# Joint projection of V and the global queries in the second layer as a 2x2 scheme of seven products

## The chip, the cores and the metric

The kernel runs on one core of a Trainium2 chip. Time is device time in microseconds, from the first to the last instruction of one execution and what lies around it. The engines are TensorE (PE in the profile: matmuls; PEld its weight loads), VectorE (DVE), ScalarE (ACT), GpSimd (POOL) and SyncE (SP), which here issues nearly all DMA transfers.

## The reference

Two layers of an encoder trunk over 512 tokens of width 1024. Each layer adds three things to x: a mixer, a cross attention over 256 memory tokens, and a gated feed-forward part with a convolution of width 3. Only the mixer's projection is touched by the change:

```python
def hybrid_mixer(h, w_in, rpb, q_norm, k_norm, w_out, rows, cos, sin):
    proj = h @ w_in                       # h = rms_norm(x), (512, 1024) @ (1024, 2304)
    na_q, na_k, na_v, g_q, g_k, g_v = jnp.split(proj, IN_SPLIT_POINTS, axis=-1)
    na_out = neighbourhood_attention(na_q, na_k, na_v, rpb, rows)
    g_q = apply_axial_rope(rms_norm(g_q, q_norm), cos, sin)
    g_k = apply_axial_rope(rms_norm(g_k, k_norm), cos, sin)
    gqa_out = gqa_block_attention(g_q, g_k, g_v)
    return jnp.concatenate([na_out, gqa_out], axis=-1) @ w_out
```

na_q, na_k, na_v and g_q have 512 columns each, g_k and g_v 128 each. All is float32.

## The kernel before, in words

**Precision.** A float32 operand is split in two parts, hi (a rounded copy, made on ACT) and lo (the remainder, a subtraction on DVE or POOL). A product is three matmuls: hi x hi, hi x lo, lo x hi (`mm3`, L650).

**Order of the work.** Each engine operation is first recorded on a tape in program order. A planner (`Tape.run`, L270, `Tape.plan`, L373) then lists the operations anew for each engine by estimated costs and due times; TensorE may run ahead of the recorded order within a reach of 300 of its instructions, tiles of the tags mm, r, t and s may be opened somewhat out of order, and all others (raw, hi, lo, sc, tr) only in order. The planner's model knows that some operations of DVE and POOL hold each other up (`Step.shared`, L337 to L340).

**Weights.** `weights()` (L1835) lists all blocks in the order of use. `get_w` (L616) keeps loads ahead: three buffers for raw blocks (N_RAW), four each for hi and lo (N_W). `emit_split` (L591) turns a raw block into hi and lo; its letter says how: "P" takes the remainder on POOL, "D" on DVE, "A" only keeps the raw block for its successor, "B" forms the combinations of the feed-forward scheme. A block is 512 KB.

**Mixer of the second layer.** The last matmuls of the first layer's feed-forward part write x, and `Norm` (L758) keeps x times the gain as hi and lo in two tiles of the tag xg; the norm's factor itself is applied later. `project_qk` (L948) projects pairs of heads, in the order of `NA_ORDER` (L50): q0, k0, q1, k1, then V, then q2, k2, q3, k3. Between q0 and k0 the statistics of the norm are begun (`mix.stat`, L793), after k0 the factor is spread over all rows (`mix.spread`, L804), and only then the first results leave PSUM. `project_v` (L1006) holds x as the stationary operand and streams the weights, 512 columns at a time: four blocks of 128 tokens, 8 chunks of the input width, three matmuls each. `gqa_project_q` (L1199) does the same for the global queries, later, behind `gqa_project_kv`; each block then goes through `head_norm` (L1147), rotation and a transpose.

All projections are pieces of a filler (`Filler`, L1377). `attn_fill.step(N_FIRST[l])` (L1381) runs the first 22 pieces in the second layer ahead of everything else: q0, k0, q1, k1 and six pieces of V. The rest is woven between the steps of the neighbourhood attention (`weave`, L1395; 2050 ns of TensorE work at each of three places of a step, NA_FILL), and then between those of the global attention (L1402). The output projection of the neighbourhood half opens once the last of its heads is there.

**Buffers.** PSUM has four banks of the tag mm, two of sc, two of tr. SBUF has 23 tiles of the tag r and 14 of the tag t.

**A scheme of the same kind** is there already: the feed-forward part computes gate and value with seven products of half size in place of eight (`operands`, L1557, `up`, L1603), with 128 x 128 weights as the stationary operand.

Of the kernel before, what the change touches and what calls it, by code (L numbers as in the profile page):

```python
# [14 lines left out]
ALU = mybir.AluOpType  # L15
# [4 lines left out]
P = 128  # L20
# [34 lines left out]
NA_FILL = 2050  # L55
# [4 lines left out]
N_RAW, N_W, AHEAD, AHEAD_HELD, N_WARM, N_LATE, N_FIRST = 3, 4, 2, 5, 7, 4, (12, 22)  # L60
# [121 lines left out]
class Tape:  # L182
# [87 lines left out]
    def run(self, due, rank, patience, ahead, margin=0.0, aside={}, order=None, rng=None):  # L270
# [32 lines left out]
        for _ in steps:  # L303
            best = None
            for e in ENGINES:
# [194 lines left out]
def encoder_kernel(ctx: ExitStack, tc: tile.TileContext, t: dict, out: list):  # L500
# [5 lines left out]
    LO_A, SUMS, LO_S = DVE, POOL, DVE  # L506

# [44 lines left out]
    done = [0]  # L552

# [37 lines left out]
    def emit_split(act=ACT, cuts=2):  # L591
# [10 lines left out]
        raws[n] = None  # L602
        if key[0] in ("up", "down", "memq", "memo"):
            cuts = 1
# [85 lines left out]
    def load_parameters():  # L690
        SP.dma_start(par, t["par"])
        taps = par[:, :, CW : CW + 6 * NF].rearrange("p l (i s j) -> p l i s j", i=3, s=2)
        for i in range(DEPTH):
            DVE.tensor_scalar(minus[:, i].rearrange("p (i j) -> p i j", i=3), taps[:, i, :, 1], -1.0, None, op0=ALU.mult)
        SP.dma_start(qkg, t["qkg"])
        SP.dma_start(gcol, t["gcol"])
# [215 lines left out]
    for l in range(DEPTH):  # L912
# [201 lines left out]

        gq, gr, gk, gvt, gtab = [None] * NB, [None] * NB, [], [None] * NB, []
# [31 lines left out]
        def head_norm(x, n, which, b):  # L1147
# [7 lines left out]
            if which:  # L1155
                DVE.scalar_tensor_tensor(view(v), view(v), 1.0 / HD, geps[:, 1, b].unsqueeze(2).to_broadcast([P, 2, 2]),
                                         op0=ALU.mult, op1=ALU.add)
            else:
                DVE.tensor_scalar(v, v, geps[:, 0, b : b + 1], None, op0=ALU.add)
# [217 lines left out]
        attn_fill = Filler(  # L1377
            PE, late, *([project_first(), *units[3:]] if l == 0 else units), gqa_project_kv(), gqa_project_q(),
# [7 lines left out]
        def na_quanta(s):  # L1386
# [4 lines left out]
            if s == 3:  # L1391
                gqa_tables()
            return [NA_FILL] * 3

# [158 lines left out]
        H = S // 2  # L1553
# [281 lines left out]
def weights():  # L1835
# [14 lines left out]

    def pair(j):
# [9 lines left out]
    for l in range(DEPTH):  # L1861
        for n, p in NA_ORDER:
            if n == "v":
# [6 lines left out]
        blocks += wide("gq", "w_in", 1536)  # L1870
# [95 lines left out]
```

## Time and profile before

| | |
|---|---|
| median of 2 runs | 1301.22 us (1300.8 to 1301.65) |
| the profiled execution's own time | 1302.85 us |
| its span in the profile | 1300.8 us |
| mean granted TensorE clock | 0.998 |
| TensorE matmuls | 7557 |
| DMA | 137.48 MB, mean 106 GB/s |
| HBM read and written | 126.18 MB and 2.10 MB |

A line of a timeline has the start in us, the duration, engine, line of the kernel, operation, the tile written and those read, shapes, and the count of merged instructions; in brackets the idle time before it and what ended it. Since the tape plays all operations at one place, every instruction has the line L405; one goes by the names of tiles. In a group of instructions the columns behind the bar are busy time in us and the mean in ns, and behind the second bar idle time before them. In the list of waits stand the engine and tile that waited, what it waited for, and then total us, times, and the longest. Durations of neighbouring instructions on an engine overlap by some tens of ns, so the distance of their starts is what one costs.

### The profile page before, as it was taken

How to read it: one execution, taken by the hardware profiler on the slowest of the kernel's cores; microseconds unless marked ns; L12 is line 12 of the kernel's file. 1: busy time of each engine (PE TensorE's matmuls, PEld its weight loads, DVE VectorE, ACT ScalarE, POOL GpSimd, SP SyncE). 2: the span in 40 equal slices, each digit the busy share in tenths (PEclk: the TensorE clock that was granted, in tenths of full speed). 3: DMA queues.
4: the chain of work that ended last, by engine and by line, in shares of the span. 5: the costliest groups of instructions: out<-in, count | busy, mean ns of one | idle time of the engine just before them, and what ended most of it. 6: DMA issues, size and time to landing. Idle time of an engine off the chain costs nothing.

```text
span 1300.8 us, 20807 instructions
## 1 busy us (share of the span) xinstructions
PE 1290.8 (99%) x7557; PEld 1138.5 (88%) x7557; DVE 1076.1 (83%) x2001; ACT 784.4 (60%) x1526; POOL 659.5 (51%) x527
## 2 busy tenths in 40 slices
PE   9999999999999999999999999999999999999998
PEld 7898888888899999999888988888888999999997
DVE  7689885769999999888555897956799999997884
ACT  7776786555665555554537866865646555554552
POOL 4565857716823534433726566765365333452360
PEclk9999999999999999999999999999999999999999
DMA  8741313313224333223355322232132233323231
GB/s 286 224 141 49 105 56 98 98 35 113 81 82 123 105 113 115 66 98 123 112 162 179 115 80 82 65 99 96 49 98 81 82 115 115 128 99 98 97 99 66
DMA packets 42902, 137.48 MB, mean 106 GB/s; under 512 B 5040, under 2 KB 8496, under 8 KB 42800
## 3 DMA queue, kind: packets, MB, share of 16 engines
q1 hardware_dynamic: 42224, 135.51, 32.9%
q8 instruction: 59, 0.97, 0.3%
q10 hardware_dynamic: 576, 0.66, 0.1%
q14 instruction: 43, 0.35, 0.1%
HBM read 126.18 MB, written 2.10 MB: 99 GB/s over the span
## 4 chain that ended last, share of the span: by engine, by line
PE 91%; DVE 5%; issue 2%; POOL 2%; ACT 1%; DVEq 0%; POOLq 0%; ACTq 0%
PE mm L405 52%; PE tr L405 20%; PE sc L405 19%; DVE t L405 2%; DVE r L405 1%; POOL lo L405 1%; DVE lo L405 0%; DVE s L405 0%; POOL s L405 0%; POOL t L405 0%; ACT r L405 0%; ACT t L405 0%; DVE mm L405 0%; DVE xg L405 0%; DVE hi L405 0%
## 5 line engine op out<-in xcount | busy, mean ns | idle before, releaser
L405 POOL TENSOR_TENSOR lo<-raw,hi 128x512 fp32r<-128x512 f32 (+2 forms) x164 | 255.9, 1579 | 161.6 <-ACT hi L405 153.9
L405 PE MATMUL mm<-xg,hi 128*128 128x512 f32 (+1 forms) x930 | 289.7, 392 | 0.0
L405 POOL TENSOR_TENSOR t<-raw,raw 128x512 f32<-128x512 f32 x64 | 99.1, 1569 | 284.2 <-DMA raw<-in_w 231.1
L405 ACT CAST hi<-raw 128x512 fp32r<-128x512 f32 (+2 forms) x212 | 159.6, 779 | 109.2 <-issue 37.2
L405 PE MATMUL mm<-r,hi 128*128 128x512 f32 (+1 forms) x704 | 222.0, 388 | 0.0
L405 PEld LDWEIGHTS mm<-xg,hi 128*128 128x128 f32 x930 | 170.8, 189 | 31.9
L405 PE MATMUL mm<-xg,lo 128*128 128x512 f32 (+1 forms) x465 | 181.3, 390 | 0.0
L405 PEld LDWEIGHTS mm<-r,hi 128*128 128x128 f32 x704 | 130.2, 188 | 25.9 <-DVE xg L405 0.8
L405 PE MATMUL mm<-r,lo 128*128 128x512 f32 (+1 forms) x384 | 141.5, 369 | 0.0
L405 PE MATMUL sc<-r,r 128*128 128x256 f32 (+1 forms) x760 | 133.9, 309 | 0.0
L405 PE MATMUL sc<-r,hi 128*128 128x256 f32 (+1 forms) x832 | 122.9, 291 | 0.8 <-DVE hi L405 0.8
L405 PEld LDWEIGHTS sc<-r,hi 128*128 128x128 f32 x832 | 109.0, 192 | 3.6 <-DVE hi L405 1.0
L405 PEld LDWEIGHTS sc<-r,r 128*128 128x128 f32 x760 | 106.0, 191 | 6.3 <-ACT t L405 0.6
L405 PE MATMUL tr<-r,lo 128*128 128x256 f32 (+1 forms) x784 | 108.9, 285 | 0.0
L405 PE MATMUL mm<-hi,xg 128*128 128x512 f32 (+1 forms) x384 | 108.1, 357 | 0.0
L405 POOL TENSOR_TENSOR t<-t,raw 128x512 f32<-128x512 f32 x64 | 102.7, 1605 | 5.0
L405 PEld LDWEIGHTS mm<-xg,lo 128*128 128x128 f32 x465 | 87.5, 188 | 18.2
L405 POOL TENSOR_SCALAR t<-t,s 128x512 f32<-128x512 f32 (+1 forms) x112 | 66.9, 611 | 71.7 <-DVE s L405 68.4
L405 PE MATMUL tr<-r,r 128*128 128x256 f32 x768 | 102.7, 283 | 0.0
L405 PEld LDWEIGHTS tr<-r,r 128*128 128x128 f32 x768 | 98.9, 191 | 2.6
L405 PEld LDWEIGHTS tr<-r,lo 128*128 128x128 f32 x784 | 99.7, 192 | 0.8
L405 DVE TENSOR_TENSOR r<-raw,r 128x512 fp32r<-128x512 f32 x96 | 91.3, 956 | 0.2 <-ACT r L405 0.2
(160 smaller groups left out, 2697.3 us busy)
## 6 DMA issues: line engine op xcount, KB each, us to landing
raw<-in_w SPq DMA_DIRECT2D x207, 512.0 KB, 3.5
r<-r SPq DMA_DIRECT2D x30, 256.0 KB, 3.6
r<-in_bias SPq DMA_DIRECT2D x16, 384.0 KB, 4.6
raw<-in_w SPq DMA_DIRECT2D x8, 384.0 KB, 3.1
r<-in_memT SPq DMA_DIRECT2D x4, 512.0 KB, 6.7
xT<-in_w SPq DMA_DIRECT2D x7, 256.5 KB, 4.5
r<-in_w SPq DMA_DIRECT2D x9, 128.0 KB, 4.1
t<-in_memT SPq DMA_DIRECT2D x4, 256.0 KB, 6.1
```

The source lines that it names most:

```text
L405: call(*args, **kwargs)
```

## The change

In the second layer alone, V (512 columns) and the global queries (512 columns) are computed together. The tokens are cut in two halves, the input width in two halves, and the columns in V and queries. Of this 2x2 product of 2x2 blocks, seven products of block size are taken in place of eight. Each has two blocks of 128 tokens by 512 columns, over four chunks of the input width. The left-hand names are combinations of weight blocks, the right-hand ones of blocks of x: 11 x 11, s1 x t1, s2 x t2, 12 x 21, s4 x 22, s3 x t3, 22 x t4, in this order. The sums of weights are made on DVE: s1 and s3 from two freshly loaded raw blocks, s2 and s4 by adding one raw block to the sum before. Blocks 11, 12, 21 and 22 of the weights are therefore loaded more than once: 18 loads in place of 8. The combinations of x are made after the norm's factor is known and include it, so V and the queries need it no more. The queries come out with the opposite sign, which the gain of the second layer takes up.

V and queries now both lie among the first 36 pieces (with four pieces of q2) ahead of the weaving; the queries' place behind the keys falls away in the second layer. The tables of the rotation are made ahead of the operands in both engines' lists, rather than in step 3 of the weaving. The planner's rule for operations that DVE and POOL can't run side by side is changed for both layers: such an operation may now start only when the other engine's is nearly over.

```diff
-N_RAW, N_W, AHEAD, AHEAD_HELD, N_WARM, N_LATE, N_FIRST = 3, 4, 2, 5, 7, 4, (12, 22)
+N_RAW, N_W, AHEAD, AHEAD_HELD, N_WARM, N_LATE, N_FIRST = 3, 4, 2, 5, 7, 4, (12, 36)
...
-                        can.append((max(t, ready[i], free[e]), i))
+                        t = max(t, ready[i], free[e])
+                        if not order and steps[i].shared:
+                            t = max(t, (vector if e == E_POOL else pool) - GRACE)
+                        can.append((t, i))
...
+    SUM7, LO7 = DVE, DVE
...
+        if eng[0] in "SC":
+            q = key[1]
+            if key[0] == "s1":
+                chain[q] = [tmp() for _ in range(2)]
+            other = raws[n - 1] if eng[0] == "S" else None
+            for k in range(2):
+                c = chain[q][k]
+                SUM7.tensor_add(c, raw[:, k], c if other is None else other[:, k])
+            if other is not None:
+                raws[n - 1] = None
+            hi, lo = wtile("hi").rearrange("p (k c) d -> p k (c d)", k=2), wtile("lo").rearrange("p (k c) d -> p k (c d)", k=2)
+            for k in range(2):
+                act.copy(hi[:, k], chain[q][k])
+                LO7.tensor_sub(lo[:, k], chain[q][k], f(hi)[:, k])
+            ready.append((hi, lo))
+            return
...
+        def operands7():
+            for n in ("11", "21", "22"):
+                hl = [rtile((4, H)) for _ in range(2)]
+                right[n] = [tuple(v[:, c] for v in hl) for c in range(4)]
+            for c in range(4):
+                one, two = tmp((2, H)), tmp((2, H))
+                xs = []
+                for k in (c, c + 4):
+                    v = tmp()
+                    DVE.scalar_tensor_tensor(v, xT[k], par[:, l, G_MIX + k : G_MIX + k + 1], mix.rep, op0=ALU.mult, op1=ALU.mult)
+                    xs.append(v)
+                a, b = xs
+                for n, v in (("11", a[:, :H]), ("21", b[:, :H]), ("22", b[:, H:])):
+                    hi, lo = right[n][c]
+                    ACT.copy(hi, v)
+                    DVE.tensor_sub(lo, v, f(hi))
+                POOL.tensor_sub(one[:, 0], a[:, :H], a[:, H:])
+                DVE.scalar_tensor_tensor(one[:, 1], one[:, 0], -1.0, b[:, H:], op0=ALU.mult, op1=ALU.subtract)
+                POOL.tensor_sub(two[:, 0], b[:, H:], a[:, H:])
+                DVE.scalar_tensor_tensor(two[:, 1], one[:, 1], -1.0, b[:, :H], op0=ALU.mult, op1=ALU.subtract)
+                hi, lo = rtile((4, H)), rtile((4, H))
+                for n, v in ((0, one), (2, two)):
+                    ACT.copy(hi[:, n : n + 2], v)
+                    DVE.tensor_sub(lo[:, n : n + 2], v, f(hi[:, n : n + 2]))
...
+            x, v = [ps_mm() for _ in range(2)], [ps_mm() for _ in range(2)]
+            yield from product(x, "11", "11", True)
+            p1 = kept(x)
+            yield from product(v, "s1", "t1", True)
+            p5 = kept(v)
+            yield from product(x, "s2", "t2", False)
+            u2 = kept(x)
+            y = [ps_s() for _ in range(2)]
+            yield from product(y, "12", "21", True)
...
+            for i in range(2):
+                DVE.tensor_add(p1[i], y[i], p1[i])
+                values(i, p1[i])
+            yield from product(v, "s4", "22", False)
+            for i in range(2):
+                DVE.tensor_add(v[i], v[i], u2[i])
+                values(2 + i, v[i])
+            straddle(vs)
+            yield from product(x, "s3", "t3", False)
+            for i in range(2):
+                DVE.tensor_add(p5[i], x[i], p5[i])
+                queries(2 + i, p5[i])
+            yield from product(x, "22", "t4", False)
+            for i in range(2):
+                queries(i, x[i])
...
-        units = [project_v() if n == "v" else project_qk(n, p) for n, p in NA_ORDER]
+        units = [(project_seven() if l else project_v()) if n == "v" else project_qk(n, p) for n, p in NA_ORDER]
+        if l:
+            units.insert(4, prepare7())
...
+        loads = [load("11", "11", q, "D") for q in range(2)]
+        for name, a, b in (("s1", "22", "21"), ("s2", "11", None), ("12", "12", None), ("s4", "12", None),
+                           ("s3", "11", "21"), ("22", "22", None)):
+            for q in range(2):
+                if b:
+                    loads += [load(name + "a", a, q, "A"), load(name, b, q, "S")]
+                else:
+                    loads.append(load(name, a, q, "D" if name in corner else "C"))
```

`product` takes, for each of two weight blocks, two chunks and two token blocks, the three matmuls; `kept` copies two banks to SBUF on ACT; `values` splits a block of V into hi and lo; `queries` does the norm, the rotation and, later, the transpose of a block. `prepare7` makes the tables and the operands and stands behind k1.

More of the change, by code (lines that the diff above doesn't have):

```diff
@@ L552, in encoder_kernel @@
     done = [0]
+    chain = [None] * 2
     def raw_tile():
@@ L695, in load_parameters @@
         SP.dma_start(qkg, t["qkg"])
+        for i in range(1, DEPTH):
+            DVE.tensor_scalar(qkg[:, i, 0], qkg[:, i, 0], -1.0, None, op0=ALU.mult)
         SP.dma_start(gcol, t["gcol"])
@@ L1157, in head_norm @@
                                          op0=ALU.mult, op1=ALU.add)
+            elif normal:
+                DVE.tensor_scalar(v, v, 1.0, EPS * HD, op0=ALU.mult, op1=ALU.add)
             else:
@@ L1862, in weights @@
         for n, p in NA_ORDER:
-            if n == "v":
+            if n == "v" and l:
+                blocks += seven()
+            elif n == "v":
                 blocks += wide("v", "w_in", 1024, "DPDP")
@@ L1869, in weights @@
             blocks.append(cols(("gkv", kh), "w_in", 4 * kh, 4, 2048, 256))
-        blocks += wide("gq", "w_in", 1536)
+        if not l:
+            blocks += wide("gq", "w_in", 1536)
         for mp in range(4):
```

58 lines of the change are left out of this document (52 added, 6 removed).

## The prediction

> **What bounds the kernel now.** I read the page's first two parts, then the waits of TensorE, then a table by stage of the second layer's attention.
>
> ```profile
> span 1300.8 us, 20807 instructions
> PE 1290.8 (99%) x7557; PEld 1138.5 (88%) x7557; DVE 1076.1 (83%) x2001; ACT 784.4 (60%) x1526; POOL 659.5 (51%) x527
> DVE  7689885769999999888555897956799999997884
> GB/s 286 224 141 49 105 56 98 98 35 113 81 82 123 105 113 115 66 98 123 112 162 179 115 80 82 65 99 96 49 98 81 82 115 115 128 99 98 97 99 66
> ```
> ```profile
> PE tr L405 <- DVE s L405: 1.2, 1, 1.2
> PE sc L405 <- DVE hi L405: 0.8, 1, 0.8
> ```
>
> TensorE has work all the way: its longest single wait is 1.2 us. So a matmul taken out is worth its whole pitch, as long as nothing new keeps the next one waiting. The engine behind it is VectorE, 83% busy, but unevenly: its digits fall to 5 in slices 20 to 22 (618 to 715 us), where the second layer begins and where the change lies. The table cuts that layer at the first matmul of (q,1), at the place where the last of the seven products would ideally begin, and at about the beginning of the global attention:
>
> ```profile
> 660.40:704.00 43.60, 43.60 (x216) 36.83 (x216) 21.35 (x52) 25.32 (x59) 17.77 (x20) 1.00 0.61 175
> 704.00:780.00 76.00, 76.00 (x462) 67.37 (x461) 65.29 (x160) 54.26 (x133) 47.02 (x48) 1.00 0.35 108
> 780.00:850.00 70.00, 69.53 (x381) 58.21 (x380) 59.87 (x137) 55.45 (x122) 48.36 (x52) 1.00 0.25 76
> ```
>
> The columns are the stretch, its length, busy time of PE, weight load, DVE, ACT, POOL, then the granted clock (1.00 throughout), the DMA share and GB/s. VectorE is idle for 22.3 us of the first stretch, 10.7 of the second and 10.1 of the third: 43.1 us in all. The question is whether the new VectorE work fits there, and in time.
>
> **What is removed from TensorE.** V and the queries now take the forms of x as the stationary operand:
>
> ```profile
> L405 PE MATMUL mm<-hi,xg 128*128 128x512 f32 x128 | 41.5, 393 | 0.0
> L405 PE MATMUL mm<-lo,xg 128*128 128x512 f32 x64 | 25.1, 392 | 0.0
> ```
> ```profile
> 672.39 0.61 PE L405 MATMUL mm<-hi,xg 128*128 128x512 f32 x2
> ...
> 681.24 0.61 PE L405 MATMUL mm<-hi,xg 128*128 128x512 f32 x2
> ```
>
> That is 192 matmuls of 512 columns. Between the two starts lie 13 groups of three, so the pitch is 8.85 / 39 = 0.227 us. The seven products are 7 x 4 chunks x 2 token blocks x 3 = 168 of the same shape and operand roles, so the same pitch. Saved: 24 x 0.227 = **5.45 us**. Nothing else of TensorE's work changes.
>
> **What VectorE gets.** Its prices come from the existing scheme at the head of the first layer's FFN, and from the splits at the head of the second layer:
>
> ```profile
> 318.86 0.74 DVE L405 SCALAR_TENSOR_TENSOR t<-xT,par,tr 128x512 f32<-128x512 f32 x1
> 319.51 2.52 DVE L405 TENSOR_TENSOR r<-t,r 128x512 fp32r<-128x512 f32 x1
> ...
> 337.93 0.42 DVE L405 SCALAR_TENSOR_TENSOR t<-t,t 128x256 f32<-128x256 f32 x1
> 338.26 0.87 DVE L405 SCALAR_TENSOR_TENSOR t<-mm,par,t 128x504 f32<-128x504 f32 x2
> ```
> ```profile
> 360.57 0.68 DVE L405 TENSOR_TENSOR r<-t,r 128x512 fp32r<-128x512 f32 x1
> 361.17 0.68 DVE L405 TENSOR_TENSOR t<-t,t 128x512 f32<-128x512 f32 x1
> 361.77 0.68 DVE L405 TENSOR_TENSOR r<-t,r 128x512 fp32r<-128x512 f32 x1
> ```
> ```profile
> 654.77 0.69 DVE L405 TENSOR_TENSOR lo<-raw,hi 128x512 fp32r<-128x512 f32 x1
> ...
> 656.69 0.26 DVE L405 TENSOR_SCALAR geps<-s 128x4 f32<-128x4 f32 x2
> 660.47 0.72 DVE L405 STREAM_TRANSPOSE rep<-tr 128x512 f32<-128x512 f32 x1 [3.52 <-PE tr L405]
> 661.22 0.70 DVE L405 TENSOR_TENSOR sc<-sc,rep 128x512 f32<-128x512 f32 x1
> 661.83 0.69 DVE L405 SCALAR_TENSOR_TENSOR sc<-sc,rep 128x512 f32<-128x512 f32 x1
> 663.76 2.11 DVE L405 TENSOR_TENSOR r<-sc,r 64x512 fp32r<-64x512 f32 x3 [1.24 <-ACT r L405]
> 666.02 0.70 DVE L405 SCALAR_TENSOR_TENSOR mm<-mm,rep 128x512 f32<-128x512 f32 x1
> ```
>
> From start to start a two-input pass over 512 columns in SBUF takes 0.60 us (361.17 to 361.77), the scaled pass over x 0.65 (318.86 to 319.51), a pass over 256 columns 0.33 (337.93 to 338.26), a half-partition split out of PSUM 2.11 / 3 = 0.70. I use these.
>
> operands7 has 8 scaled passes (5.2 us), 20 passes over 256 columns (three remainders and two sums for each of four chunks, 6.6) and 8 remainders over 512 (4.8): 16.6 us. The weights have 14 blocks of two halves, each half with a remainder (28 passes), and 8 of them with an addition in each half (16): 44 x 0.60 = 26.4 us. The six additions out of PSUM cost some 0.70 each, 4.2 us. What goes is the remainder of V's two "D" blocks, 4 x 0.60 = 2.4 us. The value splits and the queries' norm and rotation stay. Net: 16.6 + 26.4 + 4.2 - 2.4 = **44.8 us more on VectorE**, against 43.1 us idle up to 850.
>
> The hard part is time. operands7 multiplies by the norm's spread row, which VectorE writes at 660.47 and not earlier. By the start of the last product it must have done:
>
> - the spread row and the splits of the first four projections, since their PSUM banks are wanted again (by the product 12 and by s1): 0.75 + 0.61 + 0.69 + 2 x 0.70 + 8 x 0.70 = 9.1 us;
> - operands7, 16.6 us;
> - the weights, 44 passes less the first block's two, which fit ahead of 660 as V's first block does at 654.77, and less the last block's two: 40 x 0.60 = 24.0 us;
> - the two additions that read x between s3 and 22, 1.4 us.
>
> That is 51.1 us. VectorE is idle for the 3.52 us before the spread row. Only additions of raw weights could go there, and with three raw buffers of which two still hold the blocks for 11, I credit 0.8 us (bounds 0 and 3.5): 50.3 us. TensorE reaches V at 671.26:
>
> ```profile
> 671.26 0.39 PE L405 MATMUL mm<-hi,xg 128*128 128x512 f32 x1
> ```
>
> Six products of 24 make 32.7 us, so it could begin the last at 703.9, which is 43.4 us after 660.5. VectorE is late by 50.3 - 43.4 = **6.9 us**. Nothing of weight fills the gap: weight buffers are handed out strictly in order, so (q,2) can't overtake the seven, and scores of the neighbourhood attention need the sc banks that 12 holds, and VectorE itself.
>
> **POOL beside it.** operands7 gives POOL eight subtractions, and POOL slows VectorE:
>
> ```profile
> 317.82 1.30 POOL L405 TENSOR_TENSOR r<-t,r 128x512 fp32r<-128x512 f32 x1 [5.11 <-PE mm L405]
> 319.09 2.40 POOL L405 TENSOR_TENSOR lo<-raw,hi 128x1024 fp32r<-128x1024 f32 x1
> ...
> 323.15 0.74 POOL L405 TENSOR_TENSOR t<-t 128x256 f32<-128x256 f32 x1
> ```
>
> The VectorE remainder at 319.51 took 2.52 us instead of 0.68 beneath the POOL pass of 2.40: 0.77 us lost for each us of POOL. The scaled pass at 318.86, which has one input in PSUM, lost nothing beside the POOL pass of 317.82. Eight passes of 0.74 are 5.9 us: 0 to 4.5 us of delay. The planner's new rule, which starts such passes later rather than against each other, argues for less than the worst; I take **2.3 us**.
>
> The Trainium skill (GPSIMD Engine Reference, 8. Key points) says that GpSimd shares its SBUF interfaces with VectorE, in contention with VectorE instructions that have two SBUF inputs. The row at 319.51 agrees. Nearly all added passes are of that kind; were the two engines wholly exclusive, the 5.9 us would count in full, and the sum below would be 1308.6.
>
> **Costed at nothing.** ACT:
>
> ```profile
> L405 ACT CAST hi<-raw 128x512 fp32r<-128x512 f32 x61 | 35.7, 623 | 22.8 <-PE sc L405 8.1 <-PE mm L405 4.3 <-issue 3.8
> ```
>
> It gains 12 weight casts, 20 operand casts and 6 copies out of PSUM, at most 38 x 0.62 = 23.6 us on its 25.3 of the first stretch: 48.9 us, under VectorE's 50.3 + 2.3, and the softmax of that stretch moves behind the seven. It is next if VectorE were relieved. DMA: 18 blocks of 512 KB in place of 8 are 9.4 MB; over the 52 us that the seven and (q,1), (k,1) then take it is 181 GB/s, where the first slice shows 286. SP issues ten more loads. POOL loses 12 remainders of weights, for which TensorE did not wait; relief for VectorE from that is not credited.
>
> **The sum**, against the profiled execution's 1302.85 us: 1302.85 - 5.45 + 6.9 + 2.3 = 1306.6. The median of the runs shown is 1.63 below that execution: **1305.0 us**. This assumes that what VectorE has put off (values, queries, additions) finds its place behind the seven: its work from 660.4 to 850 is 21.35 + 65.29 + 59.87 + 44.8 = 191.3 us, the stretch then has 189.6 - 5.45 + 9.2 = 193.4. It just fits.
>
> **Rivals.**
>
> *TensorE stays fed* (the planner hides all). For: in slices 10 to 16 VectorE shows nines and TensorE does not wait. Against: 50.3 us due in 43.4. It would need the 3.5 us before 660.5, no contention, and splits put off. Then 1301.2 - 5.45 = 1295.8; half hidden, about 1300.
>
> *VectorE's excess is carried on.* From 660.4 to 780 VectorE has 21.35 + 65.29 = 86.6 us now and 131.4 then, while TensorE needs 119.6 - 5.45 = 114.2. If none of it slips past the beginning of the global attention, that point comes at 660.4 + 131.4, 11.8 us later than now, even with VectorE never idle: 1301.2 + 11.8 = 1313.0. It decides from the point at which the neighbourhood softmax, which VectorE carries, leaves TensorE nothing that may run ahead: V and the queries, so far its filler, are then used up. For: VectorE is at 86% there already. Against: the planner may pull the output projection forward, and after 780 there are 10 us free.
>
> *The loads.* s1 and s3 need two raw blocks for each 2.7 us of TensorE, through three buffers. The page's median over all loads, then the loads from 600 to 760:
>
> ```profile
> raw<-in_w SPq DMA_DIRECT2D x207, 512.0 KB, 3.5
> ```
> ```profile
> DMA to landing us min/median/max: 2.9/3.6/6.8
> ```
>
> With 3.6 us to land and some 2.6 until a buffer is free, 18 blocks take 18 / 3 x 6.2 = 37 us and are hidden; with 6.8 they take 56, and TensorE loses about 56 - 43 = 13 us, less 5.45: 1309.
>
> *It is the planner's rule that counts.* It changes the order everywhere; TensorE's whole idle time is 10.0 us, so little can be won and a few us lost elsewhere: 1298 to 1308.
>
> **How the numbers follow.** Forecast (TensorE starved by a few us, 1300 to 1308) 0.45; fed 0.28; carried on 0.17; loads 0.05; planner alone 0.05. The forecast's own range is 1300.0 (idle before the spread row fully used and no contention, 1305.0 - 2.7 - 2.3) to 1307.2 (worst contention). The range for 8 in 10 takes in the fed case and most of the carried one: 1295.5 to 1315. Two per cent, about what a measurement of this kernel can tell from no change, is 26 us: no case goes there. Faster 0.01, within 0.96, slower 0.03.
>
> **What would show it.** Right: TensorE's matmul count falls by 24; DVE's busy time rises by about 45 us; TensorE waits on DVE for 7 to 10 us in total between the first of the seven and the last, on operands (xg's successors in r) and on weights (hi, lo), with VectorE at 9 in those slices; the page's PE idle grows from 10 to 17 or more. Wrong: TensorE's waits stay at about 4 us and the span falls by 5; or the waits lie on raw loads; or they lie after the seven, in the neighbourhood softmax.

## The result, and the profile after the change

The changed kernel takes **1332.67 us** (median of two runs, 1331.51 to 1333.84); the kernel before took 1301.22. The ratio is 1.0238, with a 95% interval of 1.0222 to 1.0254: slower by 31 us. The forecast was 1305.0 us, in a range of 1295.5 to 1315.0. The mechanism that the prediction named is there, but it is only one of two, and the other, which is at least as large, it costed at nothing: the hole that the queries leave at the end of the neighbourhood attention.

One sentence on the change has to be put right first. Of the 36 pieces that are emitted ahead of the weaving none belongs to q2. Each of the seven products gives four pieces, so the 36 are q0, k0, q1 and k1 (16), the operands (1) and 19 pieces of the seven: 11, s1, s2, 12 and three quarters of s4. Behind them, as filler for the neighbourhood attention, remain 54 matmuls of the seven (54 x 0.227 = 12.3 us), the four projections q2 to k3 (96 x 0.227 = 21.8) and the global attention's keys and values (11.5), 45.6 us. Before, there were 13.6 us of V, the same 21.8 and 11.5, and 21.8 of the queries: 68.7.

From the first two parts of the changed kernel's page (PEclk is the granted clock of TensorE in tenths, slice by slice):

```profile
span 1332.1 us, 20904 instructions
PE 1297.4 (97%) x7533; PEld 1138.5 (85%) x7533; DVE 1082.9 (81%) x2084; ACT 803.3 (60%) x1564; POOL 644.7 (48%) x523
DVE  7688885678999988786699975956689999987784
PEclk9999999999999999999989998999999999999999
```

TensorE has 24 matmuls less, as it should, and yet its busy time is 6.6 us longer, and its idle time is 1332.1 - 1297.4 = 34.7 us where it was 10.0. A matmul that takes longer is one at a lower clock: slices 20 and 24 (666 to 699 us, 799 to 833 us) show an 8 there. The waits of TensorE, which were all under 1.3 us before, name the places:

```profile
PE mm L408 <- DVE t L408: 7.3, 6, 1.9
PE mm L408 <- ACT r L408: 4.6, 1, 4.6
PE sc L408 <- ACT t L408: 3.5, 4, 1.2
PE mm L408 <- DVE r L408: 3.5, 3, 2.3
PE mm L408 <- ACT hi L408: 3.4, 2, 3.0
```

Then the table by stretches (length, busy time of PE, weight load, DVE, ACT, POOL, granted clock, DMA share, GB/s), first the three of the prediction, then three of the changed kernel's own: the products, the neighbourhood attention, and its end up to the global attention's first scores.

```profile
660.40:704.00 43.60, 35.16 (x136) 26.94 (x135) 43.17 (x76) 24.79 (x49) 9.61 (x10) 0.88 0.44 132
704.00:780.00 76.00, 72.35 (x434) 62.12 (x434) 68.14 (x167) 57.47 (x141) 41.33 (x42) 1.00 0.64 192
780.00:850.00 70.00, 62.88 (x322) 52.74 (x321) 51.66 (x126) 44.99 (x105) 39.19 (x43) 0.93 0.24 76
671.00:711.00 40.00, 31.56 (x120) 23.93 (x119) 39.67 (x69) 22.01 (x43) 3.88 (x5) 0.87 0.49 154
711.00:780.00 69.00, 65.35 (x404) 56.32 (x403) 61.17 (x156) 53.89 (x135) 41.33 (x42) 1.00 0.65 193
780.00:814.00 34.00, 27.35 (x124) 22.63 (x123) 21.09 (x55) 17.72 (x45) 16.31 (x18) 0.85 0.22 64
```

There are two places with two different faces. From 671 to 711 us VectorE works 39.67 of 40 us and TensorE is idle for 8.4: the products starve on VectorE. The clock of 0.87 over 40 us is worth up to 5.2 more. From 780 to 814 us VectorE is idle for 12.9 of 34 us and TensorE for 6.6, with a clock that costs up to 5.1: nobody is the bound there, a chain is. Together with 3.6 us of idle time between them these are some 29 us. Another 5.7 us of idle time lie behind, from 814 to 1000 us, where the kernel before has none.

TensorE's timeline shows the first place (start, duration, tile, shape, count; in brackets the idle time before and its releaser):

```profile
674.96 0.40 PE L408 MATMUL mm<-hi,r 128*128 128x512 f32 x1
679.99 0.80 PE L408 MATMUL mm<-hi,r 128*128 128x512 f32 x1 [4.63 <-ACT r L408]
680.58 0.63 PE L408 MATMUL mm<-lo,r 128*128 128x512 f32 x1
681.00 0.63 PE L408 MATMUL mm<-hi,r 128*128 128x512 f32 x1
681.43 0.63 PE L408 MATMUL mm<-lo,r 128*128 128x512 f32 x1
...
689.65 0.73 PE L408 MATMUL mm<-hi,r 128*128 128x512 f32 x2 [3.00 <-ACT hi L408]
...
691.13 0.63 PE L408 MATMUL mm<-hi,r 128*128 128x512 f32 x1
691.56 0.63 PE L408 MATMUL mm<-lo,r 128*128 128x512 f32 x1
...
720.95 0.47 PE L408 MATMUL mm<-hi,r 128*128 128x512 f32 x1 [0.24 <-DVE t L408]
```

Product 11 has the operands of its first three chunks and waits 4.63 us for those of the fourth. ScalarE's rounding is the releaser, but it waits for VectorE's scaled pass. Behind that wait the matmuls start every 0.43 us (681.00 to 681.43) and not every 0.227: half clock. The Trainium skill (TensorE: Matmul & The Clock Gate, Part 1) says that the clock falls from 2.4 to 1.2 GHz after an idle window of about 3.4 us; this place agrees. The second wait, of 3.00 us, is followed by the same pitch of 0.43 us. The last product starts at 720.95.

And the second place:

```profile
796.25 0.71 PE L408 MATMUL mm<-r,r 128*128 128x256 f32 x4 [1.00 <-DVE t L408]
798.41 0.71 PE L408 MATMUL mm<-r,r 128*128 128x256 f32 x4 [1.45 <-DVE t L408]
801.06 1.19 PE L408 MATMUL mm<-r,hi 128*128 128x512 f32 x2 [1.94 <-DVE t L408]
802.04 0.63 PE L408 MATMUL mm<-r,lo 128*128 128x512 f32 x1
802.47 2.33 PE L408 MATMUL mm<-r,hi 128*128 128x512 f32 x5
...
813.98 1.07 PE L408 MATMUL sc<-r,r 128*128 128x512 f32 x4
```

These are values of the last units (mm<-r,r), each waiting for an addition of VectorE, and then the output projection (mm<-r,hi), which waits for one too and goes on at half clock (802.04 to 802.47). The last line shown is the first score of the global attention. In the kernel before, the queries' products ran between the last units' values, from 744 to 772 us, and the first score of the global attention came 35.5 us earlier:

```profile
778.45 1.17 PE L405 MATMUL sc<-r,r 128*128 128x512 f32 x4
```

### The profile page after: what moved, and what is told of

It is laid out like the page before. It is cut to its first block, busy times and chain, and to the rows that moved or that the text cites. A ratio compares the mean times of both kernels' runs of the same rounds, so it can differ in the third digit from the quotient of the medians.

```text
span 1332.1 us, 20904 instructions
## 1 busy us (share of the span) xinstructions
PE 1297.4 (97%) x7533; PEld 1138.5 (85%) x7533; DVE 1082.9 (81%) x2084; ACT 803.3 (60%) x1564; POOL 644.7 (48%) x523
## 4 chain that ended last, share of the span: by engine, by line
PE 82%; DVE 13%; ACT 2%; issue 2%; DMA 1%; SPq 0%; POOL 0%; ACTq 0%; DVEq 0%; POOLq 0%
PE mm L408 48%; PE sc L408 18%; PE tr L408 17%; DVE t L408 4%; DVE r L408 4%; DVE lo L408 1%; ACT t L408 1%; DVE hi L408 1%; DMA raw<-in_w 1%; DVE sc L408 1%; ACT r L408 1%; DVE mm L408 0%; DVE s L408 0%; ACT hi L408 0%; DVE xg L408 0%
## 5 line engine op out<-in xcount | busy, mean ns | idle before, releaser
L408 POOL TENSOR_TENSOR lo<-raw,hi 128x512 fp32r<-128x512 f32 (+2 forms) x152 | 240.9, 1603 | 190.9 <-ACT hi L408 184.5
L408 POOL TENSOR_TENSOR t<-raw,raw 128x512 f32<-128x512 f32 x64 | 93.2, 1478 | 301.6 <-DMA raw<-in_w 209.7
L408 POOL TENSOR_TENSOR t<-t,raw 128x512 f32<-128x512 f32 x64 | 99.9, 1562 | 5.0
L408 ACT ACTIVATE t<-sc,s,s 128x512 f32<-128x512 f32 (+1 forms) x96 | 68.1, 711 | 27.3 <-DVE s L408 25.7
L408 PEld LDWEIGHTS mm<-r,lo 128*128 128x128 f32 x384 | 72.8, 190 | 12.9
```

Source lines behind the costliest of these rows:

```text
L408: call(*args, **kwargs)
```

## The experiments

Times are compared by their ratio to the kernel before on the same chip. The brackets behind a ratio hold its 95% interval; 0.001 is 1.3 us. A figure "+20.6" is (ratio - 1) x 1301.2 us. The changed kernel stands at +31.0. Theory at the outset: the cost has a part from VectorE's work and a part from the place of the queries; the rival was that VectorE's work, or the planner's new rule, is all of it.

**The rule alone, and the change without the rule.** The rule is the line that lets an operation shared between VectorE and POOL start only when the other's is nearly over.

```diff
+                        if not order and steps[i].shared:
+                            t = max(t, (vector if e == E_POOL else pool) - GRACE)
...
```

> The kernel before with the planner's new rule for operations that DVE and POOL can't run side by side, and nothing else of the change. Theory: the 31 us come from the scheme's place in the second layer (VectorE short of time in the seven products, then a bare tail of the neighbourhood attention), not from the rule: 1298 to 1304 us, and VectorE's busy time falls by some 30 us since passes no longer run against POOL. Rival (the rule reorders everything and is what costs): above 1315 us.

> The changed kernel with the planner's old rule. Theory: 1327 to 1338 us, as slow as the changed kernel or a little slower, since more passes collide with POOL. Rival (the rule is what costs): below 1312 us.

The kernel before with the rule: 1299.97 us, ratio 0.9985 [0.9973, 0.9996], -2.0. The changed kernel without it: 1338.6 us, 1.0284 [1.0254, 1.0314], +37.0, 6.0 us more than with it, though the two intervals touch. So the rule does not cost anything; it is a small gain in both. It also explains why VectorE's busy time rose by only 6.8 us: without the rule it is 1122.9 us, 46.8 more than before (44.8 were forecast); with it VectorE's passes are shorter. Two groups of the kernel before, and then of the changed one:

```profile
L405 DVE TENSOR_TENSOR r<-raw,r 128x512 fp32r<-128x512 f32 x96 | 91.3, 956 | 0.2 <-ACT r L405 0.2
L405 DVE TENSOR_TENSOR hi<-t,hi 128x512 fp32r<-128x512 f32 x64 | 64.3, 1005 | 10.7 <-ACT hi L405 10.7
```
```profile
L408 DVE TENSOR_TENSOR r<-raw,r 128x512 fp32r<-128x512 f32 x96 | 79.2, 842 | 2.6 <-ACT r L408 2.6
L408 DVE TENSOR_TENSOR hi<-t,hi 128x512 fp32r<-128x512 f32 x64 | 52.7, 823 | 9.7 <-ACT hi L408 9.7
```

The same passes take 842 ns for 956 and 823 for 1005. It is the rule that does this: in the changed kernel without it they take 989 and 995.

**The move alone.** The kernel before, in which the second layer projects the queries right behind V, with plain products and the old rule. As in the change, more pieces run ahead of the weaving, 38 in place of 22:

```diff
-N_RAW, N_W, AHEAD, AHEAD_HELD, N_WARM, N_LATE, N_FIRST = 3, 4, 2, 5, 7, 4, (12, 22)
+N_RAW, N_W, AHEAD, AHEAD_HELD, N_WARM, N_LATE, N_FIRST = 3, 4, 2, 5, 7, 4, (12, 38)
...
+        if l:
+            units[4:5] = [tables_first(), project_v(), gqa_project_q()]
...
```

> The kernel before, in the second layer with the tables and the global queries placed right behind V (plain products, 192 matmuls, no combinations), and the first 38 pieces ahead of the weaving, so that about as much TensorE work as in the changed kernel is left for the weaving. The planner's old rule. Theory of two places: the queries are missing as filler behind the keys, TensorE idles at the tail of the neighbourhood attention as at 780 to 801 us in the changed kernel, and its clock halves: 1308 to 1320 us. Rival (all of the loss comes from VectorE's extra passes, the tail being late only because VectorE was): 1299 to 1304 us, no waits there.

1320.29 us, 1.0143 [1.0114, 1.0173]: **+18.6** with not one operation more. The table, from (q,0) on:

```profile
648.00:702.00 54.00, 54.00 (x242) 44.76 (x241) 20.18 (x34) 19.03 (x33) 24.29 (x20) 1.00 0.56 151
702.00:770.00 68.00, 66.00 (x415) 58.87 (x413) 54.70 (x148) 51.46 (x132) 41.18 (x43) 1.00 0.42 140
770.00:801.00 31.00, 24.52 (x107) 20.28 (x107) 19.98 (x48) 16.13 (x38) 13.79 (x16) 0.79 0.13 34
```

TensorE is never idle up to 702, where it has the queries. The loss is at the attention's end: 6.5 us of idle time in 31, and a clock of 0.79. With the queries and the greater count of pieces ahead of it, the attention also begins later. Its first scores in the kernel before, and then in this one:

```profile
682.14 1.12 PE L405 MATMUL sc<-r,r 128*128 128x256 f32 x8
```
```profile
702.35 1.11 PE L405 MATMUL sc<-r,r 128*128 128x256 f32 x8
```

So the move takes filler from the attention's end and puts the same work ahead of its beginning. The count of pieces was never varied alone, so what the move would cost with 22 pieces ahead is not known.

**The hole filled with work that nobody needs.** The kernel with the move alone, with 96 matmuls of the queries' size as filler where the queries were:

```diff
+        def again():
+            for b in range(NB):
+                pm = ps_mm()
+                for k in range(KC):
+                    mm3(pm, *(v[:, b * P : b * P + P] for v in xg[k]), *xg[k], k == 0, k == KC - 1)
+                    if k % 2 == 1:
+                        yield
...
-            PE, late, ..., gqa_project_kv(), *([] if l else [gqa_project_q()]),
+            PE, late, ..., gqa_project_kv(), *([again()] if l else [gqa_project_q()]),
```

> The kernel with the move alone (queries right behind V, plain products, 1320.3 us) with 96 matmuls of the queries' size added as filler where the queries' were, their sums read by nobody: 21.8 us of TensorE more than any kernel needs. Theory (the move costs by the hole that it leaves at the attention's end): the hole takes most of them, 1320 to 1327 us. Rival (the move costs by something else, and TensorE's time just adds up): 1335 to 1342 us.

1327.67 us, 1.0195 [1.0181, 1.0209], +25.4: just above the theory's range and far from the rival's. The added 21.8 us of TensorE cost 25.4 - 18.6 = 6.8; some 15 us of them went into the hole (both intervals together leave about 4 us either way). The same three stretches:

```profile
648.00:702.00 54.00, 53.60 (x238) 43.79 (x237) 21.48 (x34) 18.89 (x32) 23.89 (x20) 1.00 0.54 146
702.00:770.00 68.00, 68.00 (x424) 60.75 (x423) 53.68 (x144) 50.02 (x127) 41.30 (x43) 1.00 0.43 140
770.00:801.00 31.00, 30.64 (x163) 25.75 (x162) 25.02 (x60) 20.28 (x52) 13.48 (x17) 1.00 0.15 42
```

In the last one TensorE is busy for 30.64 of 31 us, at full clock, and VectorE gets more done than without the filler (25.02 against 19.98). So most of what the move costs, some 15 of the 18.6 us, is time in which TensorE has nothing that it may run. This is shown, not only argued: work put into that time costs little.

**Weights off VectorE.** The changed kernel without the sums of weight blocks (ScalarE copies one raw block in their place), and with ScalarE's copies for the remainders of the summed blocks:

```diff
-                SUM7.tensor_add(c, raw[:, k], c if other is None else other[:, k])
+                if other is not None:
+                    act.copy(c, raw[:, k])
...
-                LO7.tensor_sub(lo[:, k], chain[q][k], f(hi)[:, k])
+                act.copy(lo[:, k], chain[q][k])
```

> The changed kernel in which VectorE does no sums of weights and no remainders of the eight summed blocks: ACT copies the raw block in their place (the sums and those remainders are left out of the computation). VectorE loses 32 passes of 0.60, 19.2 us, ACT gains 24 of about 0.58. Theory of two places: the 16 us lost inside the seven shrink to 4 or less, the tail stays: 1314 to 1322 us. Rival (VectorE's excess alone): 1296 to 1306 us. If neither place hangs on VectorE's weight passes: above 1327 us.

A miss: 1333.55 us, 1.0245 [1.0215, 1.0275], +31.9, with 32 passes less on VectorE (19.2 us by the price of 0.60; its busy time fell by 13.1). The products end 4.7 us earlier, but the first stall is still there (4.29 us), the first scores come only 1.9 us earlier and the last ones hardly (0.7 us). So VectorE's weight work alone is not what costs.

**All of VectorE's new work off.** Besides the weights' sums and remainders, this kernel leaves out the combinations of x: each token operand is one rounded copy of x (times the gain) by ScalarE, used for both parts. With that the norm's factor in the operands, POOL's eight subtractions and half of the 14 operand tiles go too.

```diff
-                    DVE.tensor_sub(lo, v, f(hi))
...
+                    ACT.activation(right[n][c][0], xT[k][:, s], AF.Copy, scale=par[:, l, G_MIX + k : G_MIX + k + 1])
...
```

> The changed kernel, with VectorE's work for the scheme left out: no sums and remainders of token operands (each is a plain rounded copy of one input, used for both parts) and none of the summed weights (copies by ScalarE). The matmuls and transfers are those of the change, the values are not. Theory (VectorE's queue of some 50 us starves the seven products, 13.6 us of idle time and half clock, and 3.6 us more in the neighborhood attention behind it): the seven products run through without a stall and the time is 1313 to 1319 us. Rival (the loss sits in the order of the work, with nothing left to fill the attention's end): the seven products end 13 us earlier and all of it is given back behind, 1328 to 1334 us.

1321.19 us, 1.0158 [1.0141, 1.0175], +20.6. The seven run through, busy for 33.88 of the 34 us from 671 to 705, and the first scores start at 698.1 and not at 711.3, 13.2 us earlier. But only 10.4 come out at the end. Between theory (1313 to 1319) and rival (1328 to 1334): the loss is real and the end takes some of the gain back.

**The debt, and the filler's spread.** While its next piece is not allowed to run, the filler goes on adding up what it owes. When the output projection is freed, it then pays in one block ahead of the global attention. Struck out:

```diff
+        if self.forgets and self.closed():
+            self.owed = 0.0
...
-        while None in gq:
-            if attn_fill.closed():
+        while None in gq or l and not gk:
+            if attn_fill.closed() or l and late.todo:
                 late.force()
...
```

The second part sees to it that the global attention's keys are turned before that attention begins.

> The changed kernel, with the filler's debt of the neighborhood attention struck out while it has nothing to give, so that the 73 matmuls of the first half's output projection come between the units of the global attention and not in one block ahead of it. Theory (the block of 16.6 us holds the first scores of the global attention back until 814 us, while VectorE idles): the first global score near 800 us, the stage behind it longer by less than is gained, 1325 to 1329 us. Rival (the block only covers a chain that is late anyway): 1331 to 1335 us.

1329.34 us, 1.0216 [1.0201, 1.0232], +28.1. The first global score comes at 804.96 and not at 813.98. The time is between the theory's range and the rival's: 2.9 us less than the changed kernel, with intervals that overlap, so a gain is likely but not shown. To this the spread is added. The spread alone did not build, so it has no time, and what it does is read against the run just told:

```diff
-            return [NA_FILLS[l]] * 3
+            return [NA_FILLS[l] if l == 0 or s < 4 else 1900 if s < 6 else 950] * 3
```

> Both of the last two: filler spread over the ten steps, and the output projection's pieces between the units of the global attention. If each does what its theory says, 1318 to 1324 us; if neither, 1331 to 1335 us.

1321.74 us, 1.0158 [1.0143, 1.0173]: **+20.6**, 10.4 us of the 31.0 by changing nothing but the order. Filler spread and no debt together are called the mended order from here on. The stretches of this kernel:

```profile
671.00:711.00 40.00, 31.63 (x122) 23.74 (x121) 39.67 (x70) 22.02 (x42) 3.37 (x5) 0.91 0.51 157
711.00:780.00 69.00, 64.71 (x403) 56.08 (x401) 63.21 (x165) 55.88 (x141) 41.44 (x44) 1.00 0.61 188
780.00:800.00 20.00, 17.10 (x86) 12.65 (x87) 15.65 (x40) 13.44 (x34) 11.28 (x12) 1.00 0.29 80
```

The products starve as before. In 780 to 800 TensorE is idle for 2.9 us, and in the changed kernel for 5.6 with a clock of 0.91. Over the whole execution TensorE's idle time is 1319.0 - 1294.7 = 24.3 us where it was 34.7, and its busy time is 2.7 us shorter, at a mean clock of 0.997 for 0.991. So most of the gain is idle time, and the smaller part is clock. Of the idle time 5.7 us lay from 814 to 1000 us in the changed kernel, where this one has none.

**The same order for the move alone, and for the change without VectorE's work.** The edits are those above, put together.

> The kernel before, with the queries projected right behind V by plain products (the earlier run with the move alone took 1320.3 us), and the filler that is left spread over the ten steps, with no debt. Theory (the move costs what it does because the attention's end has no filler; it lost about 15 us in idle time and half clock between 740 and 801 us): 1309 to 1314 us. Rival (the move costs in another way, by tiles that are held longer): 1317 to 1322 us.

> The changed kernel without VectorE's work for the scheme (values wrong in the way told for the run before with that), and with the filler spread and no debt. If VectorE's starved products and the bare end are two separate losses of 11 us each, 1308 to 1313 us. If both are one and the same loss seen at two places, 1317 to 1321 us.

1314.69 us, 1.0105 [1.0090, 1.0120], +13.7, and 1310.22 us, 1.0073 [1.0058, 1.0088], +9.5. The first is just above the theory's range: 4.9 of 18.6 us come back, the rest stays: against the kernel before TensorE is still idle for 6.0 us more (16.0 for 10.0), and busy for 6.0 us longer with the same matmuls. The second is in the range of two separate losses: 20.6 - 9.5 = 11.1 us with the mended end, 10.4 without.

**Operands alone.** From here on, but for the last run, each kernel is the changed one with the mended order (+20.6). The token operands are taken off VectorE and the weights stay; then only their order is changed; then they are off again, but with all 14 tiles filled, by ScalarE.

```diff
-                    xs.append(v)
...
-                    DVE.tensor_sub(lo[:, n : n + 2], v, f(hi[:, n : n + 2]))
+                    ACT.activation(hi[:, n : n + 2], xT[k].rearrange("p (n h) -> p n h", n=2), AF.Copy, scale=...)
```

> The changed kernel with filler spread and no debt (1321.7 us), with VectorE's work for the token operands alone left out (plain rounded copies of one input, used for both parts); the sums and remainders of the weights stay with VectorE. Leaving out both took it to 1310.2 us. If the first stall, on the operands of product 11, is what costs: 1311 to 1315 us. If it is VectorE's whole queue ahead of the last product, of which the weights are 26 of 43 us: 1316 to 1319 us. If the weights alone: 1320 to 1323 us.

> The changed kernel with filler spread and no debt (1321.7 us), with product 11's operands written ahead of all the others', so that the planner ranks them first; the same work in all. If the order at the head costs (4.6 us of idle time at 675 to 680 us, and half clock behind it): 1316 to 1319 us. If VectorE's queue as a whole sets when the last product and the scores start, or the planner goes by due times in any case: 1320 to 1324 us.

> Like the run without the token operands on VectorE (1307.9 us), which also used 7 operand tiles in place of 14; here all 14 are taken and filled, both parts by ScalarE as plain rounded copies. If VectorE's work is what costs: 1307 to 1313 us (ScalarE has some 10 us more to do in a stretch in which it is half idle). If the tiles that the operands hold (14 of 23) are what costs: 1317 to 1323 us.

Without operands 1307.88 us, 1.0046 [1.0032, 1.0060], +6.0: **14.6 us less**, more than without all of VectorE's work. With product 11's operands first 1324.26 us, 1.0169 [1.0154, 1.0185], +22.0: no gain, although TensorE is idle for only 5.8 us from 671 to 711 where it was for 8.4. So the order at the head does not matter, the queue does. With all tiles filled 1311.76 us, 1.0077 [1.0060, 1.0094], +10.0: 10.6 us less. So VectorE's work on the operands is worth about 10.6 of the 14.6 us. Three things go with it in these two runs and were not told apart from it: POOL's eight subtractions, the steps from VectorE to ScalarE and back in the making of each operand, and the wait for the norm's factor. The last seems to bring nothing, since ScalarE begins the operands at 663.66 and 664.54 us, after VectorE has written the factor's row (658.84 and 659.72). The other 4.0 us, with intervals that touch, are the tiles' or ScalarE's, which the run with all tiles keeps busy for 39.50 of the 40 us. The stretches of the first run:

```profile
671.00:711.00 40.00, 38.66 (x176) 31.45 (x175) 36.24 (x72) 30.80 (x61) 2.37 (x2) 1.00 0.90 244
711.00:780.00 69.00, 63.82 (x407) 55.01 (x405) 60.58 (x160) 57.28 (x149) 49.05 (x54) 1.00 0.44 141
780.00:800.00 20.00, 18.84 (x89) 15.32 (x90) 14.52 (x33) 10.77 (x23) 9.95 (x10) 1.00 0.33 92
```

176 matmuls in place of 122 in the same 40 us. VectorE is at 36.24 of 40 and no longer late, with the weights still on it.

**The weights' sums on POOL,** which is busy in 4 of these 40 us:

```diff
-    SUM7, LO7 = DVE, DVE
+    SUM7, LO7 = POOL, DVE
```

> The changed kernel with filler spread and no debt (1321.7 us), and the 16 sums of weight blocks on POOL in place of VectorE. VectorE gives up 16 operations of 0.69 to 0.75 us, 11.5 us; POOL, busy in 4 of the 40 us around the products, takes 16 of 1.3 to 1.56 us. If the two work side by side, the products end 6 to 10 us earlier and the time is 1313 to 1318 us. If a POOL operation stretches VectorE's by about its own length, or the sums come later than VectorE's did: 1321 to 1328 us.

Worse than both forecasts: 1333.14 us, 1.0250 [1.0234, 1.0265], +32.5, 11.9 more than with the sums on VectorE. Groups of this kernel from 671 to 721 us:

```profile
L408 DVE TENSOR_TENSOR lo<-t,hi 128x512 fp32r<-128x512 f32 x14 | 15.8, 1128 | 3.2 <-ACT hi L408 2.6
L408 POOL TENSOR_TENSOR t<-raw,t 128x512 f32<-128x512 f32 x8 | 12.5, 1580 | 8.3 <-DMA raw<-in_w 8.3
L408 POOL TENSOR_TENSOR t<-raw,raw 128x512 f32<-128x512 f32 x6 | 10.5, 1773 | 4.0 <-DMA raw<-in_w 4.0
L408 DVE TENSOR_TENSOR r<-t,r 128x256 fp32r<-128x256 f32 x10 | 6.2, 632 | 0.0
L408 DVE TENSOR_TENSOR lo<-raw,hi 128x512 fp32r<-128x512 f32 x4 | 4.8, 1228 | 0.0
```

VectorE's remainder of a weight takes 1128 ns where it took 686 (in the run with the mended order), the one of an operand 632 where it took 419. Over the rows shown and their counterparts these are 14 x 0.44 + 10 x 0.21 + 4 x 0.54 = 10.4 us, as much as the sums had taken there (5.7 + 5.2 = 10.9). Nothing is won on VectorE (busy for 1086.6 us over the execution where it was 1082.2, with 16 passes less), and the chain of weights now has sums of 1.6 to 1.8 us in it.

**More cover.** The global attention's keys and values ahead of the seven, and the memory's keys and values ahead of the output projection:

```diff
...
-            units.insert(4, prepare7())
+            units[4:4] = [prepare7(), gqa_project_kv()]
...
-            out_na(), memory_keys(), memory_values(),
+            *([memory_keys(), memory_values(), out_na()] if l else [out_na(), memory_keys(), memory_values()]),
...
```

> The changed kernel with filler spread and no debt, the global attention's keys and values projected ahead of the seven products (11.5 us of TensorE as cover for VectorE's operands), and the memory's keys and values ahead of the first half's output projection (21.8 us of filler for the attention's end). Theory (both losses are want of cover): 1307 to 1314 us. Rival (23 operand tiles: the memory's can only be had when V's seven are given back, so the end stays bare): 1319 to 1327 us.

1331.02 us, 1.0227 [1.0210, 1.0244], +29.5: a miss, 8.9 worse than without. TensorE is still idle for 10.4 of the 18 us from 682 to 700, and VectorE is busy in 17.86 of them; the keys and values bring work of their own for it. At the other end, 780 to 800, TensorE is idle for 6.2 us at a clock of 0.59. The time lies outside both ranges. The bare end points to the rival (the memory's operands come too late to fill it), but what holds them was not told apart.

**The rule without the debt.** The kernel before with the rule and without the debt in either layer:

> The kernel before with the planner's rule (1300.0 us) and with the debt struck out, in both layers: 1296 to 1300 us if the debt costs there too, 1300 to 1303 us if the queries' products, still open at the attention's end, leave none.

1300.07 us, 0.9986 [0.9977, 0.9995], -1.8: less than the kernel before by 0.7 to 3.0 us, and the same as the rule alone. The debt costs nothing where the queries fill the end.

## Why the prediction was wrong

**Where the 31 us are.** The move with mended order 13.7, the scheme on top of it 20.6 - 13.7 = 6.9, the order of the filler 10.4; the sum is 31.0. The 6.9 are 5.45 of matmuls and 2.0 of the rule gained and, from the runs without operands, 10.6 to 14.6 lost; that makes 3.2 to 7.2. With the 6.0 us that the rule is worth in the changed kernel it would be less; these parts are differences of runs, each good to some 2 us, and need not add up. The forecast had +3.8 us for the scheme, so 24 us of its error of some 27 are the move and the order of the filler.

**The saving** of 24 matmuls is right: 7557 became 7533. The plain and the seven-product version, both with the mended order and the latter without VectorE's work, differ by 4.2 us, where 5.45 and the rule should give some 7; the rest was not looked for.

**VectorE's amount** is right: 44.8 us forecast, 46.8 measured under the old rule. The planner's rule, which the sum left at nothing, gives 2.0 us in the kernel before and 6.0 in the changed one.

**The start of the last product** was forecast at 703.9 + 6.9 + 2.3 = 713.1 us, and is 720.95. VectorE was indeed the cause, busy for 39.67 of 40 us. What the list of work due before that point left out stands in the groups of VectorE from 671 to 721:

```profile
L408 DVE CUSTOM_DVE_ANT_0 sc<-sc,r 128x256 f32<-128x256 f32 x6 | 2.4, 448 | 0.7 <-PE sc L408 0.7
L408 DVE TENSOR_TENSOR t<-sc,t 128x512 f32<-128x512 f32 x2 | 1.4, 688 | 0.0
L408 DVE TENSOR_TENSOR r<-mm,r 128x512 fp32r<-128x512 f32 x2 | 1.4, 688 | 0.0
L408 DVE TENSOR_TENSOR t<-mm,t 128x512 f32<-128x512 f32 x2 | 1.3, 691 | 0.0
L408 DVE TENSOR_TENSOR mm<-mm,t 128x512 f32<-128x512 f32 x2 | 1.3, 694 | 0.0
```

These are the first scores of the neighbourhood attention (sc<-sc,r), V's additions (t<-sc,t and mm<-mm,t), the split of its last two blocks (r<-mm,r) and the additions out of s3 (t<-mm,t). Only those out of s3 were in the list (1.4 us). The others are 6.5 us, and the split of V's first two blocks adds 1.4: 7.9 us, which is what the start was late by against the forecast. That the two agree so well is partly luck, since other passes were dearer or cheaper than priced.

**What lateness costs** was mis-sized too. The forecast took one wait of 9.2 us at full clock. The idle time came out near that, 8.4 us between 671 and 711; but half clock adds up to 5.2, and the runs without operands price the whole at 10.6 to 14.6 us. Also, the operands decide and not the weights: the prediction added both into one queue, but without the weights' sums and remainders nothing was gained, in the changed kernel (+31.9 for +31.0) nor when the operands are off VectorE already (+9.5 for +6.0).

**The step that failed** is the one that begins "This assumes that what VectorE has put off (values, queries, additions) finds its place behind the seven", with 191.3 us of work in 193.4 us and the verdict "It just fits." A sum over 190 us says nothing about order. In the stretch from 780 to 850 VectorE had 18 us free, while TensorE was idle for 7.1 us at a clock of 0.93: both waited for a chain. And the prediction saw the queries only as matmuls with a new price. It did not ask what they had covered where they lay. They were 21.8 us of filler at the end of the neighbourhood attention, and the move of them, with about as many pieces ahead of the attention as in the change, costs 18.6 us in a kernel that has nothing else of the change. That is the larger part of the error.

**The rivals.** "VectorE's excess is carried on", at 0.17, named the point ("V and the queries, so far its filler, are then used up") and priced it only by VectorE's excess, 1313.0; the price was TensorE's hole. The loads and the planner's rule as a loss are out: VectorE, which makes the sums out of the loads, is busy for 39.67 of the 40 us and does not wait for them there, and the rule gains. The forecast's own test said that the waits might "lie after the seven, in the neighbourhood softmax", and half of them do.

**What stays open**: the 13.7 us of the move with mended order, which look like what is left of the hole (45 to 48 us of filler for a stretch that had 68.7), but no useful work was found to put there; whether fewer pieces ahead of the weaving, at 22 as before, would have kept the filler and the early scores; and the 4.0 us between operands left out and operands written by ScalarE.

## What to carry to other kernels

A projection that stands late in the order may be filler for a chain of softmax and values: before moving it, find the chain that it covers and price the hole that it leaves, not the move (here 18.6 us for 21.8 us of matmuls moved). Look also at how much later the chain then begins (here 20.2 us). Extra work of a second engine is priced by when it is due, step by step, with everything else that the engine must let in before that point; a sum of busy time over a long stretch does not show that it fits.

## What the runs showed of the hardware

TensorE's half clock came not only behind one long wait (4.63 us, then 0.43 us a matmul for 0.227; the same behind 3.00 us) but also behind three of 1.00, 1.45 and 1.94 us with a few short matmuls between them (796 to 802 us, above). None of these three reaches the window of some 3.4 us that the Trainium skill (TensorE: Matmul & The Clock Gate, Part 1) gives for an idle TensorE; little work in a window seems to be enough. Waits as short do not always do it: in the run with the filler spread and no debt, waits of 1.42, 0.90 and 0.85 us between 778 and 794 us left the clock at 1.00, and in the move with the same order the clock was 0.61 from 780 to 784 us with no wait above 1.42. Where the line lies was not measured.

POOL's passes with two inputs in SBUF stretch VectorE's remainders beside them: 1128 ns for 686, 632 for 419, while POOL's sum takes 1580 to 1773. Moving 16 passes from a saturated VectorE to an idle POOL relieved VectorE of nothing. The Trainium skill (GPSIMD Engine Reference, 8. Key points) says that GpSimd shares its SBUF interfaces with VectorE, in contention with VectorE instructions that have two SBUF inputs; the runs agree.
